# Three more block products in the first FFN of a two-layer trunk, and the side work moved for them

## The chip, the cores and the metric

The kernel runs on one core of a Trainium2 chip, in one launch. The metric is the device time of one execution in microseconds (us), the median of several runs. All arithmetic is float32; the matrix products are made of parts in a rounded format ("hi" and "lo" of each operand), three passes per product.

## The reference

Two layers, each of a mixer (attention, a convolution module and a short gated convolution side by side) and an FFN, on 528 positions (16 meta tokens and 512 inputs) of width 1024. The part that the change touches is the FFN of the first layer:

```python
def ffn_sublayer(h, pre_g, post_g, w_up, conv_w, w_down):
    u = rms_norm(h, pre_g)
    z = jnp.einsum("bld,df->blf", u, w_up)
    z = causal_depthwise_conv(z, conv_w)
    g, up = jnp.split(z, 2, axis=-1)
    y = jnp.einsum("blf,fd->bld", jax.nn.silu(g) * up, w_down)
    return h + rms_norm(y, post_g)
```

The hidden width is 2816, so `w_up` has 22 blocks of 128 columns for the gate and 22 for the other half, and `w_down` has 22 blocks of 128 rows.

## The kernel before

**Layout.** Activations lie with the features across the 128 partitions and the positions along the free side. A matmul has a 128x128 block of weights standing and at most 264 positions (half of 528) moving. Every weight block comes from DRAM by SP's queue into a `raw` buffer (three of them in a ring), is rounded by ScalarE into `whi`, and VectorE makes `wlo = raw - whi` (L652 and L653 in `prep_one`). The product of a block is whi*uhi, whi*ulo and wlo*uhi. `next_w` keeps two blocks split ahead of the one in use.

**The FFN in three parts.** The 22 pairs (gate block f and up block f) are done in parts of 8, 7 and 7 (`PARTS`). In a part, the pairs are multiplied, put through the convolution of three taps, silu and product (`ffn_gate`, which ends with VectorE's `y` at L2191), and then the part's gates go through their share of `w_down`, eight chunks of 128 columns: the part's down product. A plain pair is 96 matmuls (two blocks, 8 row blocks, 3 passes, 2 halves); a down product of the first part in the first layer is 384.

**Seven instead of eight.** Some pairs are made by `seven_pair`. Rows of weights, gate and up, and the two halves of the positions give a 2x2 by 2x2 block product, and seven products of blocks do it in place of eight: 7 x 4 row blocks x 3 passes = 84 matmuls (L2288 in `product`). They need sums of activations, four tiles `t` made by `normalised` in steps that `build` lets out during the first part (five behind each of pairs 2 to 6, in order) and during the first down product; a `None` in the steps ends a call. And they need sums of weight blocks, `w_sum` in DRAM, which are made long before the pair, in one of these ways:

- by DMA: three copies from DRAM to DRAM from SP's queue (L545), then three DMAs of POOL's queue that add into DRAM (L534), each behind the one before (`sum_steps`). In the mixer they are operations of the plan, at the lowest priority (8), with `SUM_LAT` as the planned time to landing and `SUM_EVERY` between two sums. In the FFN, `tick` lets out one step per pair.
- on VectorE, during a down product, in the tile of h as a spare (`down_sum`, L589 to L601).

Which pair is made when is in `SUMS`: for each layer five places, namely the FFN before (for layer 0 nothing), the mixer, the FFN's ticks, the first and the second down product.

**The spare.** Behind the first part h isn't needed until the FFN's end. It is copied to DRAM (`h_dram`, L2385), its tile serves as four more raw buffers, and it is read back later.

**Blocks split ahead.** While layer 0's FFN runs, six blocks of layer 1's input projection are split and put into DRAM as hi and lo, so that layer 1's mixer needn't split them. `store_one` does it in seven calls: each splits the block that the call before loaded (ScalarE L666 into `shi`, VectorE L667 into `slo`, one buffer each, then two stores from POOL's queue at L670), and all but the last load another (SP, L675). `shi` and `slo` also serve the block products.

**Order.** In the mixer and at the FFNs' ends the order on PE, ACT, DVE and POOL is written out by a planner (`Flow`) that has costs per operation; an operation with a priority number of 4 or more gives way there to one that is ready soon. In the rest of the FFN, and on SP's queue everywhere, the tile framework sets each queue's order by simulating the program, so that an instruction may be issued ahead of its place in the code; `issue_after` ties one instruction behind another of its engine. Each engine works its own queue strictly in order.

```python
for b in (b12, b22, b11, b21):
    for k in range(K2):
        yield lambda b=b, k=k: un(b, k)
for k in range(0, K2, 2):
    if k:
        yield None
```

Of the kernel before, what the change touches and what calls it, by code (L numbers as in the profile page):

```python
# [28 lines left out]
PARTS = (8, 7, 7)  # L29


SUMS = (((), (11, 12, 13), (15, 16), (17, 18), (19, 20)),
        ((8, 9), (10, 11, 12, 13), (15, 16), (17, 18), (19, 20)))
SEVEN = tuple(sorted(sum(places, ())) for places in SUMS)
NEXT_SUMS, AHEAD_SPLITS = 13, (8, 8, 9, 9, 10, 10, 11)
SUM_US, SUM_LAT, SUM_EVERY = 0.9, 9.0, 40.0
K2 = KD // 2
SB = K2 * P
AHEAD = 2
# [350 lines left out]
def tile_hybrid_trunk(ctx: ExitStack, tc: tile.TileContext, xT, wflat, pv_d, out):  # L390
# [734 lines left out]
    def mixer(l, ypool, first, close_first, spans, front, rzs, u_at):  # L1125
# [719 lines left out]

        for i, f in enumerate(sums_at(l, 1)):
            copies, *adds = sum_steps(l, f)
            tok = flow.op("sp", 2.0, copies, (Tok(flow.pe + SUM_EVERY * i),), prio=8, lat=SUM_LAT)
            for op in adds:
                tok = gp(SUM_US, op, tok, prio=8, lat=SUM_LAT)  # L1850

# [242 lines left out]
    for l in range(DEPTH):  # L2094
# [23 lines left out]
        with tc.tile_pool(name=f"fp{l}", bufs=2, reuse_waits="tile") as fp:  # L2118
# [91 lines left out]
            def normalised():  # L2210
# [39 lines left out]
                        yield lambda b=b, k=k: un(b, k)  # L2250
                for k in range(0, K2, 2):
                    if k:
                        yield None
                        yield lambda: block(0)
                        yield None
                    yield lambda: total(2, k, lambda: at(b12), lambda: at(b22))
                    yield lambda: split(2, k)
                    yield lambda: total(0, k, lambda: at(b11), lambda: at(b12))
                    yield lambda: total(1, k, lambda: at(b22), lambda: raw[0], ALU.add)
                    yield lambda: split(0, k)  # L2260
                    yield lambda: total(3, k, lambda: at(b21), lambda: raw[1])
                    yield lambda: split(1, k)
                    yield lambda: split(3, k)
# [4 lines left out]

            mul_ins, glo_ins, ghi_ins = [None], [None], {}
            ts, n_seven, primed = [], [0], set()  # L2270
            building = [None]

            def build(n):

# [64 lines left out]
            def finish_pair():  # L2339
                if late_ups:  # L2340
                    late_ups.popleft()()
# [3 lines left out]
            for part, nf in enumerate(PARTS):  # L2345
                for f in range(f0, f0 + nf):
                    if g:
                        tick(g[max(g)][0][:, :1])
                    for _ in range(AHEAD_SPLITS.count(f) if l == 0 else 0):
                        store_one()  # L2350
                    if f in seven:
                        seven_pair(f)
                        if f == seven[-1]:
                            spare[0] = None
                            with tc.issue_after(last_load[0].ins):
                                for k in range(0, KD, 2):
                                    nc.sync.dma_start(h[:, k:k + 2], h_dram[:, k:k + 2])
                        continue
                    finish_pair()
                    if seven and f == 2:  # L2360
                        building[0] = normalised()
                    for i in (2 * f, 2 * f + 1):
                        if i < len(zs):
                            continue
                        if i < FIRST["w_out"]:
                            scaled(i, [first.ps[hf, i] for hf in range(2)])
                            continue
                        w = next_w()
                        ps = mmt((6, 2)[i % 2]) if ts else mmt()
                        mm3({hf: ps[:, hf, :iws[hf]] for hf in range(2)}, w, range(KD), u_in)  # L2370
                        if ts:
                            for (a, z), hf in zip(i_spans, range(2)):
                                nc.scalar.copy(zs[i % len(zs)][:, off + a - i0:off + z - i0], ps[:, hf, :z - a])
                            continue
                        scaled(i, [ps[:, :, :H]] if i0 == 0 else [ps[:, hf, :iws[hf]] for hf in range(2)])
                    g[f] = ffn_gate(f)
                    if building[0] is not None and f < PARTS[0] - 1:
                        with tc.issue_after(mul_ins[0].ins):
                            build(5)
                finish_pair()  # L2380
                ks = list(range(nf))
                grhs = lambda b, k, hf, f0=f0: g[f0 + k][b][:, fw * hf:fw * (hf + 1)]
                if seven and part == 0:
                    for k in range(0, KD, 4):
                        nc.sync.dma_start(h_dram[:, k:k + 4], h[:, k:k + 4])  # L2385
                    spare[0] = h
                if part < len(PARTS) - 1:
                    more = down_sums(l, part)
                    for op in more.pop(-1):
                        op()  # L2390
                    for some in ((0, 1), *((m,) for m in range(2, KD))):
# [9 lines left out]
                        if building[0] is not None:  # L2401
                            with tc.issue_after(glo_ins[0].ins):
                                build(99)
                        for m, ps in zip(some, tiles):
                            if final:
                                d, src = yp[:, m, t0:], ps[:, 0, :2 * fw]
# [84 lines left out]
```

## Time and profile before

| | |
|---|---|
| time, median of 3 runs | 1263.06 us (1262.32 to 1263.31) |
| the profiled execution: time, span | 1262.1 us, 1260.4 us |
| TensorE (PE) busy | 1244.2 us, 99% of the span |
| VectorE (DVE) busy | 926.0 us, 73% |
| ScalarE (ACT) busy | 710.3 us, 56% |
| GpSimd (POOL) busy | 175.9 us, 14% |
| DMA | 206.59 MB, 164 GB/s in the mean |
| pairs made as block products | layer 0: 11, 12, 13, 15 to 20; layer 1: 8 to 13, 15 to 20 |

The span runs from the first to the last instruction of the profiled execution; its time is 1.7 us longer. In the rows, PE is a matmul, PEld its weight load, SP the queue of most DMAs; a q behind an engine's name is its queue or sequencer. "out<-in" are the program's tile names, L837 is line 837 of the kernel. An idle time in square brackets is the time that the engine stood still ahead of the row, and what ended it.

### The profile page before, as it was taken

The numbers are of one execution on the slowest core, as the hardware profiler recorded it, in microseconds if no ns is written. First come the engines' busy times: TensorE is split into PE (matmuls) and PEld (weight loads), VectorE is DVE, ScalarE is ACT, GpSimd is POOL, SyncE is SP. The second block draws the span as 40 slices with busy tenths as digits, with TensorE's granted clock in tenths as the row PEclk, the third lists the DMA queues.
The fourth block names the chain that finished last, engine by engine and source line by source line (L and its number), as shares of the span: only waits on it lengthen the run. The fifth ranks groups of instructions, "written<-read, shape, count | busy, mean of one in ns | idle before, by whom it ended". The sixth has DMA issues, their size and how long they took to land.

```text
span 1260.4 us, 24292 instructions
## 1 busy us (share of the span) xinstructions
PE 1244.2 (99%) x9554; PEld 1194.4 (95%) x9554; DVE 926.0 (73%) x1581; ACT 710.3 (56%) x1377; POOL 175.9 (14%) x360
## 2 busy tenths in 40 slices
PE   8999999999999999999999999999999999999997
PEld 8999898999999999999999988999999899989997
DVE  7887866589874776487688877756799748757954
ACT  7254576655444663476673545775554447526763
POOL 1323411001111001010003244110022000000000
PEclk9999999999999999999999999999999999999999
DMA  7267551726658755765652684547166565465611
GB/s 245 80 154 180 122 118 47 256 88 150 185 146 339 243 192 153 243 193 169 209 186 68 157 194 109 144 116 238 70 166 177 148 212 172 151 228 178 203 60 67
DMA packets 80755, 206.59 MB, mean 164 GB/s; under 512 B 8624, under 2 KB 18992, under 8 KB 80128
## 3 DMA queue, kind: packets, MB, share of 16 engines
q1 hardware_dynamic: 66976, 168.20, 42.1%
q0 software_dynamic: 13664, 36.84, 13.0%
q8 instruction: 75, 1.23, 0.4%
q14 instruction: 40, 0.33, 0.1%
HBM read 170.82 MB, written 50.60 MB: 176 GB/s over the span
## 4 chain that ended last, share of the span: by engine, by line
PE 94%; DVE 2%; ACT 1%; DMA 1%; POOL 1%; issue 0%; SPq 0%; DVEq 0%; ACTq 0%
PE psum L837 63%; PE psum L2288 17%; PE psum L1407 5%; PE psum L1671 3%; PE psum L1637 2%; PE psum L974 1%; PE psum L1593 1%; PE psum L1737 1%; PE psum L1323 1%; DMA raw<-in_w_dram 0%; POOL dm L1608 0%; DMA h<-in_x_dram 0%; DVE yp L1050 0%; DVE h L1060 0%; PE psum L1617 0%
## 5 line engine op out<-in xcount | busy, mean ns | idle before, releaser
L837 PE MATMUL psum<-y,whi 128*128 128x264 f32 (+3 forms) x1968 | 383.8, 299 | 0.8 <-DVE zs L989 0.7
L837 PEld LDWEIGHTS psum<-y,whi 128*128 128x128 f32 x1968 | 305.8, 188 | 13.7 <-DVE zs L989 0.9
L837 PE MATMUL psum<-uhi,whi 128*128 128x264 f32 (+1 forms) x1168 | 292.2, 289 | 1.5 <-ACT uhi L2069 0.8
L837 PE MATMUL psum<-ulo,whi 128*128 128x264 f32 (+1 forms) x1168 | 286.0, 284 | 0.6 <-DVE ulo L2071 0.4
L837 PE MATMUL psum<-uhi,wlo 128*128 128x264 f32 (+1 forms) x1168 | 285.3, 284 | 0.0
L837 PE MATMUL psum<-y,wlo 128*128 128x264 f32 (+3 forms) x984 | 274.0, 297 | 0.7 <-DVE wlo L793 0.7
L837 PEld LDWEIGHTS psum<-uhi,whi 128*128 128x128 f32 x1168 | 201.7, 189 | 5.9 <-issue 1.6
L837 PEld LDWEIGHTS psum<-ulo,whi 128*128 128x128 f32 x1168 | 201.8, 189 | 1.3 <-DVE ulo L2071 0.6
L837 PEld LDWEIGHTS psum<-uhi,wlo 128*128 128x128 f32 x1168 | 201.5, 189 | 0.0
L837 PEld LDWEIGHTS psum<-y,wlo 128*128 128x128 f32 x984 | 178.0, 188 | 6.4 <-DVE wlo L793 1.1
L2173 DVE SCALAR_TENSOR_TENSOR c<-zs,pv,c 128x528 f32<-128x528 f32 (+1 forms) x176 | 130.5, 756 | 21.2 <-ACT c L2171 19.9
L652 ACT CAST whi<-raw 128x1024 fp32r<-128x1024 f32 (+1 forms) x65 | 66.1, 1021 | 96.9 <-PE psum L837 74.3
L793 DVE TENSOR_TENSOR wlo<-raw,whi 128x1024 fp32r<-128x1024 f32 (+2 forms) x80 | 95.6, 1204 | 31.1 <-ACT whi L789 30.5
L789 ACT CAST whi<-raw 128x1024 fp32r<-128x1024 f32 (+2 forms) x80 | 81.7, 1030 | 26.3 <-PE psum L837 18.1
L653 DVE TENSOR_TENSOR wlo<-raw,whi 128x1024 fp32r<-128x1024 f32 (+1 forms) x65 | 76.9, 1183 | 20.9 <-ACT whi L652 20.9
L1153 DVE SCALAR_TENSOR_TENSOR cacc<-apad,pv,cacc 128x528 f32<-128x528 f32 x120 | 87.5, 771 | 0.1
L2288 PE MATMUL psum<-uhi,whi 128*128 128x258 f32 (+1 forms) x252 | 71.4, 284 | 0.0
L2288 PE MATMUL psum<-ulo,whi 128*128 128x258 f32 (+1 forms) x252 | 71.3, 283 | 0.0
L2288 PE MATMUL psum<-uhi,wlo 128*128 128x258 f32 (+1 forms) x252 | 70.8, 283 | 0.0
L2171 ACT ACTIVATE c<-zs,pv 128x528 f32<-128x528 f32 (+1 forms) x88 | 63.0, 727 | 6.8 <-DVE zs L2136 2.6
L2206 POOL COPY cols<-y 128x1 f32<-128x1 f32 x24 | 18.4, 767 | 334.7 <-ACT y L2187 334.4
L2288 PE MATMUL psum<-t,shi 128*128 128x258 f32 (+1 forms) x336 | 63.2, 283 | 0.0
(273 smaller groups left out, 2324.4 us busy)
## 6 DMA issues: line engine op xcount, KB each, us to landing
raw<-in_w_dram SPq DMA_DIRECT2D x114, 512.0 KB, 4.6
raw<-in_w_dram SPq DMA_DIRECT2D x30, 448.0 KB, 5.2
h<-in_w_dram SPq DMA_DIRECT2D x25, 512.0 KB, 4.7
raw<-w_sum SPq DMA_DIRECT2D x21, 512.0 KB, 5.2
h<-w_sum SPq DMA_DIRECT2D x21, 512.0 KB, 5.1
h<-in_w_dram POOLq DMA_DIRECT2D x16, 512.0 KB, 4.0
w_sum<-h POOLq DMA_DIRECT2D x16, 512.0 KB, 6.3
w_sum<-in_w_dram SPq DMA_DIRECT2D x26, 256.0 KB, 5.8
```

The lines of the kernel that those rows point to most:

```text
L652: nc.scalar.copy(hi[:, :sz], raw[:, :sz])
L653: last_low[0] = nc.vector.tensor_sub(lo[:, :sz], raw[:, :sz], hi[:, :sz].bitcast(F32))
L789: nc.scalar.copy(box["hi"][:, :sz], box["raw"][:, :sz])
L793: nc.vector.tensor_sub(lo[:, :sz], box["raw"][:, :sz], box["hi"][:, :sz].bitcast(F32))
L837: nc.tensor.matmul(d, lhsT=w[a][:, k, cols], rhs=rhs(b, k, hf), start=start and i == 0 and p == 0, stop=stop and i == n - 1 and p == 2)
L1153: nc.vector.scalar_tensor_tensor(conv[j], in0=src, in1=conv[j], scalar=col("a_dw_w", CK * j + i), op0=ALU.mult, op1=ALU.add)
L1407: nc.tensor.matmul(ps[:n, :nw], lhsT=(uhi, ulo)[ui][:, k, P * b:P * b + n], rhs=w[wi][:, k % 4, :], start=k == 0 and p == 0, stop=k == KD ...
L1637: nc.tensor.matmul(s, lhsT=k[:, ka:ka + kn], rhs=q[:, s0:qz], start=i == 0, stop=i == 1)
L1671: nc.tensor.matmul(acc[:, s0 - qa:qz - qa], lhsT=vals[:, b].rearrange("p h d -> p (h d)")[:, o:o + P], rhs=box["p"], start=b == 0, stop=b ...
L2171: nc.scalar.activation(dst, src[:, 2:2 + 2 * fw], AF.Copy, scale=wtap(2, t))
L2173: nc.vector.scalar_tensor_tensor(dst, in0=src[:, i:i + 2 * fw], scalar=wtap(i, t), in1=dst, op0=ALU.mult, op1=ALU.add)
L2288: nc.tensor.matmul(psum[:, bank, :n7], lhsT=w[a][:, k0 + k, :], rhs=rhs(b, k), start=start and k == 0 and p == 0, stop=stop and k == K2 - ...
```

## The change

- Layer 0's list gets pairs 8, 9 and 10. The mixer makes the sums of 8 to 12 (before: 11 to 13), the FFN's ticks those of 13, 15 and 16 (before: 15 and 16). Layer 1's list is the same.
- The seven calls of `store_one` stand at pairs 4, 5, 6 and 7 of layer 0 (one each), ahead of the first down product, and behind its first and second group of products. Before, they stood at pairs 8, 8, 9, 9, 10, 10 and 11.
- h is copied to DRAM at pairs 2 and 3, half each, in both layers. Before, behind the first part.
- `SUM_LAT` is 16 in place of 9, and the spacing of the sums is the lesser of 40 and 216 divided by their number.
- The `None` ahead of the second round of steps in `normalised` is left out once a part's pairs are done (`downs`).

```diff
-SUMS = (((), (11, 12, 13), (15, 16), (17, 18), (19, 20)),
+SUMS = (((), (8, 9, 10, 11, 12), (13, 15, 16), (17, 18), (19, 20)),
         ((8, 9), (10, 11, 12, 13), (15, 16), (17, 18), (19, 20)))
-NEXT_SUMS, AHEAD_SPLITS = 13, (8, 8, 9, 9, 10, 10, 11)
-SUM_US, SUM_LAT, SUM_EVERY = 0.9, 9.0, 40.0
+NEXT_SUMS = 13
+SUM_US, SUM_LAT, SUM_EVERY, SUM_SPAN = 0.9, 16.0, 40.0, 216.0
...
-            tok = flow.op("sp", 2.0, copies, (Tok(flow.pe + SUM_EVERY * i),), prio=8, lat=SUM_LAT)
+            tok = flow.op("sp", 2.0, copies, (Tok(flow.pe + min(SUM_EVERY, SUM_SPAN / len(sums_at(l, 1))) * i),), prio=8, lat=SUM_LAT)
...
                     if k:
-                        yield None
+                        if not downs:
+                            yield None
                         yield lambda: block(0)
...
-            building = [None]
+            building, downs = [None], []
...
-                    for _ in range(AHEAD_SPLITS.count(f) if l == 0 else 0):
+                    if l == 0 and PARTS[0] - 4 <= f < PARTS[0]:
                         store_one()
...
+                    if seven and f in (2, 3):
+                        k = 4 * (f - 2)
+                        nc.sync.dma_start(h_dram[:, k:k + 4], h[:, k:k + 4])
...
                 finish_pair()
+                downs.append(part)
...
                 if seven and part == 0:
-                    for k in range(0, KD, 4):
-                        nc.sync.dma_start(h_dram[:, k:k + 4], h[:, k:k + 4])
                     spare[0] = h
                 if part < len(PARTS) - 1:
+                    if l == 0 and part == 0:
+                        store_one()
...
+                        if l == 0 and part == 0 and some[0] in (0, 2):
+                            store_one()
```

## The prediction

> **What bounds the kernel now.** I read the page first, then the chain of waits in order of time, then busy time by stretches of the first FFN.
>
> ```profile
> span 1260.4 us, 24292 instructions
> PE 1244.2 (99%) x9554; PEld 1194.4 (95%) x9554; DVE 926.0 (73%) x1581; ACT 710.3 (56%) x1377; POOL 175.9 (14%) x360
> ...
> 276.51 134.52 PE psum L837 x1104
> 518.29 49.77 PE psum L2288 x410
> 983.08 39.83 PE psum L837 x171
> 1022.91 2.88 PE psum L2288 x24
> 1025.91 46.37 PE psum L2288 x386
> ...
> L2288 PEld LDWEIGHTS psum<-uhi,whi x252: 186/188/192, 434.4 to 1189.2; 128*128 128x128 f32 x126
> ```
>
> TensorE is busy for 99% of the span, and in both FFNs the chain is TensorE alone, in long pieces without a hole: L837 is the plain product, L2288 the block product. So a matmul taken out there is time taken out, as long as nothing else turns up late. The pieces give the pace: 134.52/1104 = 0.1219 us for a plain matmul, 49.77/410 = 0.1214 us for a block matmul of the first layer.
>
> The same pace dates the stages. The first block product of layer 0 starts at 434.4 (the last row, which tells first and last start). Before it lie pairs 8 to 10 (3x96 matmuls, 35.1 us, from 399.3), the first down product (384 matmuls, 46.8 us, from 352.5) and pairs 2 to 7 (11.7 us each, from 282.3). In these stretches:
>
> ```profile
> core 0: us, PE busy (x) PEld busy (x) DVE busy (x) ACT busy (x) POOL busy (x), PEclk, DMA share, GB/s
> ...
> 317.40:329.10 11.70, 11.70 (x98) 11.70 (x97) 9.96 (x15) 5.28 (x7) 1.52 (x3) 1.00 0.63 229
> 329.10:340.80 11.70, 11.70 (x98) 11.70 (x97) 10.69 (x15) 5.08 (x7) 2.14 (x3) 1.00 0.57 129
> 340.80:352.50 11.70, 11.70 (x98) 11.70 (x97) 10.74 (x15) 6.68 (x9) 1.36 (x2) 1.00 0.58 146
> 352.50:364.20 11.70, 11.70 (x98) 11.70 (x98) 6.75 (x9) 3.54 (x5) 1.39 (x2) 1.00 0.37 89
> 364.20:375.90 11.70, 11.70 (x99) 11.70 (x99) 11.30 (x15) 7.51 (x11) 1.15 (x2) 1.00 0.55 189
> 387.60:399.30 11.70, 11.70 (x99) 11.70 (x98) 3.68 (x3) 5.25 (x7) 1.59 (x3) 1.00 1.03 412
> 399.30:411.00 11.70, 11.70 (x99) 11.70 (x98) 4.62 (x4) 4.54 (x7) 1.60 (x3) 1.00 0.70 239
> ...
> 548.90:559.10 10.20, 10.20 (x86) 10.20 (x85) 8.86 (x13) 7.42 (x14) 1.31 (x1) 1.00 0.53 157
> ```
>
> The clock is 1.00 throughout. VectorE has about a microsecond free per pair in pairs 5 to 7 and more than half of the time at the end of the down product and in pair 8. Work is moved from the second place to the first, and that is the risk of this change.
>
> **The products.** Pairs 8, 9 and 10 of layer 0 become block products; pair 13 was one already and only its sums move. Removed: 288 x 0.1219 = 35.1 us. Added: 3 x 7 x 4 x 3 = 252 matmuls x 0.1214 = 30.6 us. Net **-4.5 us**. The two priming matmuls with ones are the same two. That twelve such pairs in this order can run without a hole is seen in layer 1, whose list is the same: its first down product ends at 983.08 + 39.83 = 1022.91, the first block product starts there, and 46 us follow with one break of 0.12 us.
>
> A block pair costs the other engines more: 3584 weight columns to split instead of 2048 and two more sums of psum. By the rows below (1.23 us for a split of 1024 columns, 0.71 for a psum step of 528) that is 1.8 + 2 x 0.4, some 2.6 us of VectorE. It lies beside TensorE, since a stretch of nothing but block pairs (548.90) has VectorE at 8.86 of 10.2 us; without that cover it would be 8 us for three pairs.
>
> **The hole before the first block product.**
>
> ```profile
> 434.47 1.05 ACT L652 CAST whi<-h 128x1024 fp32r<-128x1024 f32 x1 [0.59 <-PE psum L837]
> 436.07 0.64 ACT L2373 COPY zs<-psum 128x264 f32<-128x264 f32 x2
> 436.49 0.51 PE L2288 MATMUL psum<-t,whi 128*128 128x264 f32 x2 [0.35 <-ACT zs L2373]
> ```
>
> Today a plain pair stands just ahead of the first block pair, its last psum banks (2 and 3) are copied out behind a weight split, and the second block product waits for bank 2. After the change a down product stands there, as in layer 1, which has no such wait. **-0.4 us** (the idle time in the last row; bounds 0 and -0.4).
>
> **The six blocks split ahead** (`store_one`). Seven calls, as before: one load each but the last, then ScalarE's rounding, VectorE's rest, two stores from POOL's queue. They go from pairs 8 to 11 to pairs 4 to 7 (one each), the start of the down product and its first two steps.
>
> ```profile
> L666 ACT CAST shi<-raw 128x1024 fp32r<-128x1024 f32 x3 | 3.2, 1053 | 2.8 <-issue 2.5 <-DMA raw<-in_w_dram 0.3
> L667 DVE TENSOR_TENSOR slo<-raw,shi 128x1024 fp32r<-128x1024 f32 x3 | 3.7, 1225 | 7.0 <-DMA w_split<-slo 6.9
> L667 DVE TENSOR_TENSOR slo<-h,shi 128x1024 fp32r<-128x1024 f32 x3 | 3.7, 1224 | 7.9 <-issue 5.7 <-ACT shi L666 2.2
> ...
> 341.03 0.71 DVE L2136 TENSOR_TENSOR zs<-psum,rz 128x528 f32<-128x528 f32 x1 [0.78 <-PE psum L837]
> 352.76 0.71 DVE L2136 TENSOR_TENSOR zs<-psum,rz 128x528 f32<-128x528 f32 x1
> 358.15 0.71 DVE L2191 TENSOR_TENSOR y<-c,y 128x528 fp32r<-128x528 f32 x1 [0.70 <-ACT y L2187]
> ```
>
> Three splits fall in pairs 5 to 7: 3 x 1.23 = 3.7 us of VectorE, against 1.74 + 1.01 + 0.96 = 3.7 us free there. VectorE is then full. What is late next is pair 7's gate: its last VectorE step ends at 358.86, and the down product asks for it after 84 matmuls, at 352.5 + 10.2 = 362.7. Slack 3.8 us. If all free time is usable, VectorE is late by only the fourth split, 1.2 us; if none is, by 3.7 + 1.2 = 4.9 us. So TensorE loses 0 to 1.1 us. VectorE waits for psum rather than the reverse (0.78 at 341.03), and a psum pair has a whole chunk (5.85 us) before it is wanted again, so I take a value near the lower end, **+0.1 us**. ScalarE has half its time free. The last two splits fall in the down product, where VectorE has 5 us free at once (352.5 to 364.2).
>
> Each load now sits in the ring of three raw buffers, not in the spare one; weight loads lose one buffer of lead. Blocks are split two chunks (11.7 us) ahead of use, and a load lands in less than half of that:
>
> ```profile
> raw<-in_w_dram SPq DMA_DIRECT2D x114, 512.0 KB, 4.6
> w_split<-slo POOLq DMA_DIRECT2D x6, 512.0 KB, 6.5
> ```
>
> (KB each, median us from issue to landing). The six loads and twelve stores are 18 x 0.524 = 9.4 MB; the stretch of 387.6 moved 412 GB/s at share 1.03 with no hole in TensorE. At that rate they are 23 us of full load; spread over pair 5 to the middle of the down product (some 59 us) they add 0.39 to shares of 0.37 to 0.63: below what is carried today. Nothing charged; the price if a load or split is late after all is in the second rival.
>
> **The sums** (`w_sum`). Layer 0's mixer makes five instead of three, and SUM_LAT spaces their three POOL steps further apart, in both layers. What that costs is not seen before it is done; the nearest rows are layer 1's mixer with four and layer 0's with three, and the wait of a diagonal-matrix step on POOL that stood behind a sum's DMA:
>
> ```profile
> 49.50:214.00 164.50, 163.25 (x1216) 149.56 (x1214) 124.54 (x295) 94.54 (x246) 51.70 (x110) 1.00 0.50 119
> 675.50:840.80 165.30, 163.42 (x1219) 149.81 (x1217) 127.21 (x299) 94.88 (x245) 58.17 (x122) 1.00 0.56 131
> ...
> 115.56 0.39 PE L1617 MATMUL psum<-dm,ones_r 128*128 128x264 f32 x1 [0.43 <-POOL dm L1608]
> 742.23 0.40 PE L1617 MATMUL psum<-dm,ones_r 128*128 128x264 f32 x1 [0.98 <-POOL dm L1608]
> ...
> 200.00:220.00 20.00, 20.00 (x152) 18.41 (x151) 10.25 (x24) 12.86 (x35) 2.55 (x9) 1.00 0.12 38
> 220.00:240.00 20.00, 20.00 (x167) 20.00 (x166) 10.59 (x11) 14.07 (x22) 0.00 (x0) 1.00 0.82 281
> ```
>
> One more sum goes with 0.8 us at most. The fifth would be copied at about 210 and added up to 260, when POOL has nothing else to do. Its copies pass SP's queue ahead of the loads of h and of weights, 2 us of issue as the plan has it, which are wanted tens of microseconds later. Bounds: -1.4 us (both waits above gone) to +2.5 us (three new ones like 742's beside the 0.43). I take half of the 0.8, **+0.4 us**.
>
> **What changes nothing.** `SUM_SPAN`: min(40, 216/5) and min(40, 216/4) are both 40. The guard `if not downs`: pairs 2 to 6 take five steps each, the first run of steps has 16 + 8 = 24, so the pause falls in pair 6, where `downs` is still empty, in both layers. The copy of h, written earlier in the code, is issued early already, since outside the planned stages the order on a queue isn't the order of the code:
>
> ```profile
> 253.49 0.33 SPq L650 DMA_DIRECT2D raw<-in_w_dram  x1
> 266.52 6.02 SPq L2385 DMA_DIRECT2D h_dram<-h  x2
> 284.27 0.33 SPq L650 DMA_DIRECT2D raw<-in_w_dram  x1
> ```
>
> It lies in a stretch in which SP issues nothing else, some 80 us ahead of its place in the code (the end of pair 7, 352.5). Each at 0; if the copy moved in between weight loads, its 6 us would lie within their lead.
>
> **Sum.** -4.5 - 0.4 + 0.1 + 0.4 = -4.4 us: a span of 1260.4 - 4.4 = 1256.0. The profiled run took 1262.1 us, 1.7 beyond its span, and the median of the runs is 1263.06, another 0.96; on the median's scale **1258.7 us** (-0.35%). No change means within 0.2%, 2.5 us.
>
> **Rivals.**
>
> *VectorE stands behind the stores* (slower). `shi` and `slo` have one buffer each; the next split on VectorE waits, in order, until the last store has landed:
>
> ```profile
> 407.88 1.23 DVE L667 TENSOR_TENSOR slo<-h,shi 128x1024 fp32r<-128x1024 f32 x1 [5.66 <-issue]
> 415.54 1.22 DVE L667 TENSOR_TENSOR slo<-raw,shi 128x1024 fp32r<-128x1024 f32 x1 [2.66 <-DMA w_split<-slo]
> ...
> L534 POOL DMA_DIRECT2D w_sum<-w_sum x26: 796/844/890, 66.2 to 984.7; - x26
> ```
>
> There VectorE had nothing else to do. In pairs 5 to 7 everything behind it (psum copies, weights, gates) is late by the whole wait. Two waits like the first and the fourth split: 11.3 + 1.2 - 3.8 of slack = 8.7 us lost, 4.5 gained with the rest: +4.2, 1267.3. It turns the sign from 7.1 us of waiting on (7.1 + 1.2 - 3.8 = 4.5). Against it: the calls now come one to a pair, 11.7 us apart, and a store lands 6.5 us after issue, so it is through before the next split; before, calls came in twos. [...] Chance 0.10.
>
> *A late load or gate in the first part.* One wait of 5.66 with the fourth split: 5.7 + 1.2 - 3.8 = 3.1 us of the 4.5, so 1261.7. For it: VectorE full, a raw buffer less. Against: lead of 11.7 us. Chance 0.13, no change.
>
> *POOL's sums in the mixers.* Three waits like 742's more than now, 2.9 us in place of 0.4: 1261.2. For it: six more POOL steps in layer 0, and all steps of layer 1 at new places. Against: they yield to other work in the plan. Chance 0.12, about a third of it still faster.
>
> *More than forecast*: both waits above vanish, 1.4 and the 0.4 charged: 1256.9. Chance 0.07.
>
> *Forecast* (1257.4 to 1260.4): 0.58. Faster 0.58 + 0.07 + 0.04 = 0.69; no change 0.13 + 0.08 = 0.21; slower 0.10. The range 1256.9 to 1262.6 takes in the middle rivals and leaves out the slower one and a little below.
>
> **What would show it.** The first block product near 398 and no plain pair but 14 and 21 behind the first part; L667 once per pair from 317 on and VectorE at 11.5 of 11.7 us there, with psum copies never a chunk late. Wrong: a hole in TensorE ahead of 399 that ends with a gate or weight (stores), or more idle behind dm (sums), or h's copies elsewhere than in SP's empty stretch.

## The result and the profile after

The change made the kernel slower: 1274.92 us in the median of 4 runs (1272.62 to 1277.13) against 1263.18 for the kernel before beside it, a ratio of 1.0091 (95% interval 1.0067 to 1.0116). Forecast were 1258.7 us and a range up to 1262.6. The profiled execution took 1276.63 us, so its rows lie near the upper end of the runs. Three executions among the experiments below and beside them took 1502 to 3582 us; the ratios leave them out.

The page of the kernel after, its busy times and TensorE's granted clock in 40 slices:

```profile
span 1274.8 us, 24316 instructions
...
PE 1246.6 (98%) x9518; PEld 1195.4 (94%) x9518; DVE 931.7 (73%) x1593; ACT 716.1 (56%) x1389; POOL 184.2 (14%) x373
...
PEclk9998999999989999999999999999999999999999
```

The matmuls are the 36 fewer that were forecast (9518 against 9554), and yet PE is busy for longer and the span is 14.4 us longer. The clock row, all nines before, has two eights (slices at 96 and 351 us). The chain of waits in order of time dates the loss. First the kernel before, three rows beside those already shown:

```profile
211.37 1.57 PE psum L837 x12
...
690.09 6.95 PE psum L837 x57
...
840.79 31.19 PE psum L837 x261
```

and the kernel after:

```profile
218.72 1.57 PE psum L837 x12
...
350.83 12.13 DMA w_split<-slo
...
527.99 49.77 PE psum L2289 x410
699.75 6.95 PE psum L837 x57
...
854.83 31.19 PE psum L837 x261
```

The same piece of layer 0's mixer comes at 218.72 and not 211.37: **7.35 us** were lost before it. The third part's block products begin at 527.99 and not 518.29: 9.70 behind, so the first FFN lost 2.35 on balance (with the 5.1 us that the products are worth, shown below, **7.4 us**). Layer 1's mixer begins as late as that (699.75 against 690.09) and ends 14.04 behind (854.83 against 840.79): **4.4 us** more. Behind it nothing changes much: 14.4 at the end.

**The two mixers.** What POOL issues, and when TensorE comes back, in the timeline of after:

```profile
102.06 0.87 POOL L534 DMA_DIRECT2D w_sum<-w_sum  x1
...
104.04 0.74 POOL L534 DMA_DIRECT2D w_sum<-in_w_dram  x1
...
114.11 0.49 PE L1593 MATMUL psum<-k,q 128*16 128x16 f32 x2 [4.08 <-issue]
...
748.64 0.50 PE L1593 MATMUL psum<-k,q 128*16 128x16 f32 x2 [3.42 <-issue]
```

The same stretch before has one sum's DMA in place of two:

```profile
101.19 1.19 POOL L534 DMA_DIRECT2D w_sum<-in_w_dram  x1
```

SP issues four copies of k at some 106.8 in both. The DMA view of that stretch (KB each, median us from issue to landing), of after:

```profile
k<-pair_hi SPq DMA_DIRECT2D x4, 132.0 KB, 7.0
```

and of before:

```profile
k<-pair_hi SPq DMA_DIRECT2D x4, 132.0 KB, 2.6
```

SP's queue (q1) and POOL's (q0) in that stretch of after, with packets, MB and the share of the 16 DMA engines' time:

```profile
q1 hardware_dynamic: 1058, 2.08, 48.3%
q0 software_dynamic: 416, 0.79, 41.0%
```

With 16 us as the planned time of a step, the last step of the first sum falls to 102.06, next to the first step of the second sum. Two sums' DMAs are then in flight when k's copies are issued, these land after 7.0 us in place of 2.6, and TensorE stands for 4.08 us. Layer 1 has the same at 745.2 (3.42). For each MB that the profile counts, the sums on POOL's queue take more than twice the engines' time of SP's transfers (41.0/0.79 = 52 against 48.3/2.08 = 23).

**The first down product.** The timeline of after, POOL, ScalarE, VectorE and TensorE:

```profile
349.38 1.22 POOL L534 DMA_DIRECT2D w_sum<-in_w_dram  x1
350.83 0.58 POOL L670 DMA_DIRECT2D w_split<-slo  x1 [0.23 <-DVE slo L667]
...
359.64 1.05 ACT L666 CAST shi<-raw 128x1024 fp32r<-128x1024 f32 x1 [4.16 <-DMA raw<-in_w_dram]
...
363.04 1.23 DVE L667 TENSOR_TENSOR slo<-raw,shi 128x1024 fp32r<-128x1024 f32 x1 [5.57 <-DMA w_split<-slo]
364.18 0.70 DVE L2184 TENSOR_TENSOR c<-c,c 128x528 f32<-128x528 f32 x1
...
365.60 0.73 PE L837 MATMUL psum<-y,whi 128*128 128x264 f32 x3 [3.01 <-ACT y L2187]
367.31 0.59 PE L837 MATMUL psum<-y,wlo 128*128 128x264 f32 x1 [0.98 <-DVE wlo L653]
```

The fourth split (349.31) stands ahead of pair 5's last VectorE step (`y`, 350.45). Its store is issued 1.5 us behind a sum's DMA on POOL's queue and takes 12.1 us (the chain's 12.13). The fifth split needs `slo` and stands next in VectorE's order, so VectorE waits for 5.57 us with the rest of pair 6's gate behind it (L2184 at 364.18), and TensorE, which began the down product at 360.26 and asks for pair 6 after 18 matmuls, for 3.01 and then for 0.98. A late load has a smaller part in it: the split's other input `shi`, for which ScalarE waited 4.16 us, was ready at 359.64 + 1.05 = 360.69, and the store alone held VectorE for the 2.35 us from there to 363.04.

By the code the fifth split belongs behind the down product's first products, and two splits lie ahead of pair 6's gate. In VectorE's order it is five: the six splits run at 305.6, 324.6, 337.6, 349.3, 363.0 and 376.3, one ahead of each `y` of pairs 2 to 7 (313.0, 326.9, 339.9, 350.4, 368.5, 380.3). The framework's simulation of the program put them there.

**The clock.** Each of the three holes is paid twice. Six stretches of after, in the columns known from the prediction (PEclk is the third number from the end):

```profile
109.00:115.00 6.00, 1.92 (x14) 1.74 (x13) 1.63 (x7) 0.39 (x1) 0.27 (x1) 0.87 1.01 207
115.00:121.00 6.00, 6.00 (x31) 6.00 (x31) 2.60 (x12) 1.52 (x3) 1.16 (x4) 0.56 0.13 35
361.00:367.00 6.00, 2.32 (x17) 1.80 (x15) 3.96 (x5) 4.35 (x6) 2.33 (x4) 0.92 0.56 167
367.00:373.00 6.00, 5.69 (x26) 5.69 (x27) 6.00 (x10) 1.90 (x3) 0.07 (x1) 0.52 1.08 240
744.00:750.00 6.00, 2.58 (x18) 2.40 (x17) 1.87 (x7) 0.39 (x1) 0.51 (x2) 0.86 0.97 223
750.00:756.00 6.00, 5.58 (x39) 5.37 (x39) 3.91 (x11) 2.22 (x4) 2.29 (x4) 0.86 0.26 67
```

From 115 to 121 TensorE is busy all the time and gets 31 matmuls done; before, at a clock of 1.00, 6 us of the same stage (109 to 115) have 50. The clock lost is (0.13 + 0.44) x 6 = 3.4 us, (0.08 + 0.48) x 6 = 3.4 and (0.14 + 0.14) x 6 = 1.7: 8.5 us in all, on top of 4.1, 4.0 and 3.4 us of standing still. Together 20 us, near the 7.35 + 7.4 + 4.4 = 19.2 of the chain (in layer 1 the wait for `dm` became 0.6 us shorter, 0.42 in place of 0.98). In slices of 1 us the granted clock is 0.50 from 114 to 120, from 366 to 372 and from 749 to 751, with values between 0.50 and 1.00 in a slice just before or behind: the losses of 3.4, 3.4 and 1.7 us are some 6.8, 6.8 and 3.4 us at half clock. They don't follow the holes' length: 3.01 us, with 0.98 behind it, cost as much as 4.08, and 3.42 half of that.

### The profile page after: what moved, and what is told of

Its sections match the earlier page's. It is cut to its first block, busy times and chain, and to the rows that moved or that the text cites. A ratio compares the mean times of both kernels' runs of the same rounds, so it can differ in the third digit from the quotient of the medians.

```text
span 1274.8 us, 24316 instructions
## 1 busy us (share of the span) xinstructions
PE 1246.6 (98%) x9518; PEld 1195.4 (94%) x9518; DVE 931.7 (73%) x1593; ACT 716.1 (56%) x1389; POOL 184.2 (14%) x373
## 4 chain that ended last, share of the span: by engine, by line
PE 85%; DMA 5%; DVE 4%; issue 2%; ACT 2%; POOL 1%; SPq 0%; DVEq 0%; ACTq 0%; POOLq 0%
PE psum L837 52%; PE psum L2289 19%; PE psum L1407 4%; DMA raw<-in_w_dram 3%; PE psum L1671 3%; PE psum L1637 2%; PE psum L974 1%; DMA w_split<-slo 1%; PE psum L1593 1%; PE psum L1737 1%; PE psum L1323 1%; DVE wlo L793 1%; ACT whi L789 1%; SPq L494 0%; DMA h<-in_x_dram 0%
## 5 line engine op out<-in xcount | busy, mean ns | idle before, releaser
L837 PE MATMUL psum<-uhi,whi 128*128 128x264 f32 (+1 forms) x1072 | 273.1, 290 | 1.7 <-ACT uhi L2069 0.8
L837 PE MATMUL psum<-ulo,whi 128*128 128x264 f32 (+1 forms) x1072 | 266.8, 285 | 0.6 <-DVE ulo L2071 0.4
L837 PE MATMUL psum<-uhi,wlo 128*128 128x264 f32 (+1 forms) x1072 | 265.9, 285 | 0.0
L837 PEld LDWEIGHTS psum<-uhi,whi 128*128 128x128 f32 x1072 | 187.9, 190 | 6.3 <-issue 2.0
L837 PEld LDWEIGHTS psum<-ulo,whi 128*128 128x128 f32 x1072 | 187.9, 190 | 1.3 <-DVE ulo L2071 0.6
L837 PEld LDWEIGHTS psum<-uhi,wlo 128*128 128x128 f32 x1072 | 187.5, 190 | 0.0
L653 DVE TENSOR_TENSOR wlo<-raw,whi 128x1024 fp32r<-128x1024 f32 (+1 forms) x64 | 75.6, 1181 | 11.8 <-ACT whi L652 11.8
L2289 PE MATMUL psum<-uhi,whi 128*128 128x264 f32 (+1 forms) x288 | 81.6, 284 | 0.0
L2289 PE MATMUL psum<-ulo,whi 128*128 128x264 f32 (+1 forms) x288 | 81.4, 283 | 0.0
L2289 PE MATMUL psum<-uhi,wlo 128*128 128x264 f32 (+1 forms) x288 | 80.8, 283 | 0.0
L2289 PE MATMUL psum<-t,shi 128*128 128x264 f32 (+1 forms) x384 | 72.2, 283 | 0.0
L2206 POOL COPY cols<-y 128x1 f32<-128x1 f32 x28 | 20.3, 725 | 337.6 <-ACT y L2187 337.4
```

The lines of the kernel that those rows point to most:

```text
L653: last_low[0] = nc.vector.tensor_sub(lo[:, :sz], raw[:, :sz], hi[:, :sz].bitcast(F32))
L837: nc.tensor.matmul(d, lhsT=w[a][:, k, cols], rhs=rhs(b, k, hf), start=start and i == 0 and p == 0, stop=stop and i == n - 1 and p == 2)
L2289: nc.tensor.matmul(psum[:, bank, :n7], lhsT=w[a][:, k0 + k, :], rhs=rhs(b, k), start=start and k == 0 and p == 0, stop=stop and k == K2 - ...
```

## The experiments

"Hole" is idle time of TensorE. The kernel before took 1262.7 to 1263.8 us beside these runs.

**One part on the old kernel: the planned time of a sum's step.**

```diff
-SUM_US, SUM_LAT, SUM_EVERY = 0.9, 9.0, 40.0
+SUM_US, SUM_LAT, SUM_EVERY = 0.9, 16.0, 40.0
```

> The kernel before with SUM_LAT 16 alone: three sums in layer 0 and four in layer 1, only POOL's order differs. Theory: both mixers get their hole and half clock, +11.3 us: 1274.5. Rival (number of sums): layer 0 has no hole with three sums, at most layer 1's +4.1: 1267.3 or 1263.2.

1271.82 us, ratio 1.0060 (1.0043 to 1.0077): some 8 us from this number alone, with three sums in layer 0 and four in layer 1. Its timeline has the two steps side by side, and both holes (the second at 741). Behind the first the granted clock is 0.96 from 109 to 115 and 0.76 from 115 to 121, (0.04 + 0.24) x 6 = 1.7 us:

```profile
101.80 0.87 POOL L534 DMA_DIRECT2D w_sum<-w_sum  x1
...
103.78 0.74 POOL L534 DMA_DIRECT2D w_sum<-in_w_dram  x1
...
113.22 0.34 PE L1593 MATMUL psum<-k,q 128*16 128x16 f32 x2 [3.43 <-issue]
```

So the mixers' loss comes from the spacing, not from the fifth sum.

**The other part on the old kernel: the stores' new place.**

```diff
-                    for _ in range(AHEAD_SPLITS.count(f) if l == 0 else 0):
+                    if l == 0 and PARTS[0] - 4 <= f < PARTS[0]:
                         store_one()
...
+                    if l == 0 and part == 0:
+                        store_one()
...
+                        if l == 0 and part == 0 and some[0] in (0, 2):
+                            store_one()
```

> The kernel before with one part of the change alone: the seven calls that split weights ahead stand in pairs 4 to 7 and at the head of the first down product; sums, spacing and pairs are as before. Theory (the stores' new place makes the hole by itself, because a store waits in POOL's queue behind a sum's DMA and VectorE waits for the store): no hole in the mixers, a hole of 3 to 4.5 us at the first down product and 6.8 us at half clock behind it, so 1263.8 + 4.4 + 3.4 = about 1271. Rival (the hole needs what the three further pairs bring: the sum steps of pair 13 in the first part and the early copy of h): no hole, 1263.5 to 1264.5.

1269.16 us, ratio 1.0045 (1.0030 to 1.0060): about 6 us, and 1.8 us less than the 1271 expected, which had 3.4 us of half clock in it. (The four executions had a mean clock of 0.997 to 1.000, so they didn't all lose as much clock.) Its chain of waits has the same step as after's:

```profile
341.32 2.07 POOL w_sum L534
343.63 12.33 DMA w_split<-slo
```

The hole needs nothing of what the three pairs bring. How long a store takes varies: 3.0 us is the fastest of before, 6.5 us is the median of the `slo` stores of before, and 12.1 and 12.3 us are these two, with a sum's DMA of 512 KB just ahead in the queue.

**Undo one part of after: the spacing back at 9 us.**

```diff
-SUM_US, SUM_LAT, SUM_EVERY, SUM_SPAN = 0.9, 16.0, 40.0, 216.0
+SUM_US, SUM_LAT, SUM_EVERY, SUM_SPAN = 0.9, 9.0, 40.0, 216.0
```

> The changed kernel with SUM_LAT back at 9: the order of every engine's queue but POOL's stays as it is. Theory (two causes that add up): with 16 the third step of the mixer's first sum and the first step of its second stand within 2 us ahead of k's copies, these land late, TensorE stands still for 4.4 us in layer 0 and 3.7 us in layer 1, and its clock is at half for 6.8 and 3.4 us after; both holes go with 9, worth 7.2 + 4.1 = 11.3 us: 1263.6. Rival (it is the number of sums, five, that overloads the mixer of layer 0, not their spacing): only layer 1's hole goes, 1270.8.

1278.14 us, ratio 1.0117 (1.0096 to 1.0137), against every expectation. The two holes ahead of k go, but with five sums a new one opens at 206.8, the longest of all:

```profile
204.59 1.15 POOL L534 DMA_DIRECT2D w_sum<-in_w_dram  x1 [5.05 <-DMA w_sum<-in_w_dram]
214.72 0.85 POOL L534 DMA_DIRECT2D w_sum<-w_sum  x1 [8.97 <-DMA w_sum<-in_w_dram]
...
215.92 0.80 PE L1671 MATMUL psum<-pf,vals 128*128 128x128 f32 x2 [9.10 <-POOL pf L1651]
```

POOL waits in order for the landing of the step before (10 us, planned as 9) and holds attention's `pf` behind it. This is the event that the prediction looked for (TensorE idle behind POOL), in a size that it did not have.

**Undo the other part of after: the stores at their old places** (pairs 8, 8, 9, 9, 10, 10 and 11, the diff above backwards), alone and together with 9 us.

> The changed kernel with the calls of store_one back at pairs 8, 8, 9, 9, 10, 10, 11, SUM_LAT still 16. Theory: the hole in the first down product (4.8 us and 6.8 us at half clock after it) goes, 7.4 us: 1267.5, with the two holes of the mixers still there. Rival (the first part is late because of the sums of three more pairs, not because of the stores): the hole stays, 1274.9. Second rival (the stores in among block pairs, with one shi and slo for both, make a new hole at pairs 8 to 11): 1270 or more.

> The changed kernel with both undone: only the three more block pairs, their two sums and the inert edits are left. Theory: no hole of three microseconds, clock at 1.0 throughout, and the block products' 4.5 us are gained: 1258.7 (1257.5 to 1260.5). Rival (five sums or stores among block pairs cost what the products gain): 1263 or more.

1302.83 us, ratio 1.0306 (1.0291 to 1.0322), and 1302.99, ratio 1.0315 (1.0298 to 1.0332). Both expectations were far off: the pairs there are block pairs now, which split into the same `shi` and `slo`. The chain of the first of the two runs:

```profile
442.74 5.27 DMA w_split<-shi
...
452.31 6.67 DMA w_split<-slo
```

These two waits end in holes of 4.85 and 3.03 us. Two more, of 3.4 and 3.2 us, lie between 424 and 480, and in the 6 us from 426, 450, 456 and 476 the granted clock was 0.82, 0.52, 0.78 and 0.63. So the stores had to move once pairs 8 to 10 were block products; what failed is the place that they got.

**Fewer sums at 9 us.**

```diff
-SUMS = (((), (8, 9, 10, 11, 12), (13, 15, 16), (17, 18), (19, 20)),
+SUMS = (((), (9, 10, 11, 12), (13, 15, 16), (17, 18), (19, 20)),
...
-SUM_US, SUM_LAT, SUM_EVERY, SUM_SPAN = 0.9, 16.0, 40.0, 216.0
+SUM_US, SUM_LAT, SUM_EVERY, SUM_SPAN = 0.9, 9.0, 40.0, 216.0
```

> The kernel after with the planned time of a sum's step back at 9 us and with pair 8 plain again, so four sums in layer 0's mixer and eleven pairs as block products. Theory (five sums were too many for the mixer's stretch at 9 us, and four are not): no hole over 1.5 us in either mixer; the hole at the first down product stays (about 4.4 us and 6.8 us at half clock); products worth two thirds of 4.5: 1263.8 - 3.0 + 7.8 = about 1268.5. Rival (any sum beyond the third meets POOL's other work): a hole of 5 to 9 us in layer 0's mixer with half clock behind it, 1275 or more.

1267.43 us, ratio 1.0032 (1.0019 to 1.0045), within 1.1 us of the theory: no hole over 0.6 us in layer 0's mixer or over 1.2 in layer 1's, and the hole at the first down product stays.

**The steps of the sums kept away from the stores.**

```diff
-                    if g:
+                    for _ in range((0, 2, 2, 2, 0, 0, 0, 0)[f] if l == 0 and f < 8 else min(1, len(g))):
                         tick(g[max(g)][0][:, :1])
```

> The kernel after, with the sums' steps of layer 0's first part two in each of pairs 1 to 3 and none in pairs 4 to 7, where the stores stand. Theory (the store of pair 7 is late because it stands behind a sum's DMA in POOL's queue): the stores land in 4 to 6 us, the hole at the first down product goes with its half clock, the two mixer holes stay: 1274.9 - 7.4 = about 1267.5. Rival (the raw loads are late because loads and stores together fill the DMA engines, whoever shares the queue): the hole stays within 1 us, 1274 to 1276.

1277.54 us, ratio 1.0119 (1.0096 to 1.0142): the time fits the rival, but the timeline shows the theory's mechanism at another place. A double step stands ahead of a store there, the store takes 8.2 us, and the second split waits for it:

```profile
323.42 1.23 DVE L667 TENSOR_TENSOR slo<-raw,shi 128x1024 fp32r<-128x1024 f32 x1 [8.30 <-issue]
...
326.09 0.48 PE L837 MATMUL psum<-uhi,whi 128*128 128x264 f32 x2 [2.58 <-DVE zs L2136]
...
367.13 0.63 PE L837 MATMUL psum<-y,whi 128*128 128x264 f32 x3 [1.38 <-ACT y L2187]
```

At the fifth split VectorE no longer waits for a store, and of the 4.0 us of hole behind it 1.8 stay (1.38, and 0.39 a little later). There it waits for ScalarE, 4.62 us at 362.13, and that waits for a late `raw` load. That fits the reading of after, in which the store held VectorE for 2.35 us longer than the late load. It isn't a clean test of the shares, since TensorE is some 3 us later here and the loads had that much more time.

**Stores not in every pair.** As the run with four sums, and:

```diff
-                    if l == 0 and PARTS[0] - 4 <= f < PARTS[0]:
+                    for _ in range((4, 6, 8, 8).count(f) if l == 0 else 0):
                         store_one()
```

> As the run with four sums and 9 us, but the seven calls that split ahead stand at pairs 4 and 6, three at the first down product as after, and two at pair 8, which is plain here. Theory (the hole at the first down product comes from stores in every one of pairs 4 to 7): no hole of 3 us anywhere, no half clock, 1263.8 - 3.0 + 0.4 = about 1261.2. Rival (two stores are enough for the hole there, or pair 8's stores delay the first block products): a hole of 3 to 4 us and 3.4 or 6.8 us at half clock at one of the two places, 1266 to 1269.

1260.20 us in 10 runs, ratio **0.9979 (0.9969 to 0.9988)**: 3.1 us less than the kernel before beside it, a small gain that the interval sets apart from none. No hole over 0.9 us up to layer 1's mixer, none over 1.7 behind it. Against the run with four sums alone the stores' place is worth 1267.4 - 1260.2 = 7.2 us.

**Five sums, and the stores apart.** The next four runs keep all twelve pairs. Three have the stores at pairs 4 and 6, around the first down product's head, and in the second down product:

```diff
-                    if l == 0 and PARTS[0] - 4 <= f < PARTS[0]:
+                    if l == 0 and f in (4, 6):
                         store_one()
...
-                        if l == 0 and part == 0 and some[0] in (0, 2):
+                        if l == 0 and (part, some[0]) in ((0, 0), (0, 2), (1, 2), (1, 6)):
                             store_one()
```

They differ in the planned time of a step: 16 us as in after, 12 and 13. The fourth has 13 us and after's stores.

> The kernel after with the seven calls that split ahead at pairs 4 and 6, three at the first down product and two in the second; the planned time of a sum's step stays at 16 us. Theory (the losses are separate and add): both mixer holes stay with their half clock, the hole at the first down product goes: 1274.9 - 7.2 = about 1267.7, up to 1270. Rival: without the stores in every pair the mixers' holes are worth what they are alone in the kernel before (8.0 us), 1259.2 + 8.0 = 1267.2; much below that, the holes of after would have had a common cause.

1268.47 us, ratio 1.0052 (1.0034 to 1.0070): the down product's hole is gone (TensorE is busy for all of 361 to 373 there, at a clock of 1.00), both mixer holes stay. 6.5 us better than after.

> The kernel after with the planned time of a sum's step at 12 us, between the 9 of before and the 16 of after, and with the seven calls that split ahead at pairs 4 and 6, three at the first down product as after, and two in the second down product (at its row blocks 2 and 6). All twelve pairs stay block products. Theory (both holes come from where POOL's DMAs fall, not from the twelve pairs): with 12 us the planner puts other POOL work between a sum's DMAs ahead of k's copies and leaves no pf behind the sums; no hole over 1.5 us, no half clock, 1263.3 - 4.5 + 0.4 = about 1259.2. Rival (no spacing carries five sums; the DMA engines are full): a hole of 3 us or more in layer 0's mixer with 3.4 to 6.8 us at half clock, 1264 or more. A hole in the second down product would speak against the stores there alone.

> As the run with 12 us, but 13 us. Theory: the same, about 1259.2, as long as no two sum DMAs stand side by side ahead of k's copies; the second step of the first sum falls later than at 12, nearer to the first pair of q's copies, so up to 1 us of hole may show there. Rival (the time follows the spacing itself, 9 to 16): between the two, a k hole of 2 to 3 us in each mixer, 1263 to 1266.

1269.15 us, ratio 1.0052 (1.0036 to 1.0067), and 1267.88, ratio 1.0040 (1.0025 to 1.0055). Both theories fell: no hole over 2 us ahead of k, but one of about 4 us near the mixer's end. The chain of the run with 13 us, and the group of TensorE that came late:

```profile
227.93 9.73 DMA raw<-in_w_dram
```

```profile
217.90 1.46 POOL L534 DMA_DIRECT2D w_sum<-in_w_dram  x1
...
253.34 1.25 PE L974 MATMUL psum<-acc,om_d 128*128 128x264 f32 x2 [4.12 <-DVE acc L934]
```

The fifth sum now falls where h and the output weights are loaded, a load takes 9.73 us, and the weights behind it stay late up to the norm. That its DMAs are the cause is likely by place and time; no run took them alone away.

> The kernel after with the planned time of a sum's step at 13 us and nothing else changed. Theory (the two losses are separate and add): the mixers' holes are gone, the hole at the first down product stays: the run with 13 us and moved stores plus 7.2 us (what the same stores cost with four sums), so about 1266.4. Rival (the holes in the first part come from the mixer ending late): none at the down product, the same time as with moved stores.

1271.22 us, ratio 1.0073 (1.0047 to 1.0099): both holes are there, the mixer's end and the down product's (4.64 us, and 3.93 and 0.68). The rival is out; the 1266.4 presumed a mixer without a hole. The stores cost 3.3 us here, less than the 7.2 between the two runs with four sums; why is open.

**Each sum where none was seen to cost.** 9 us (`SUM_LAT` as before) for the first two sums of layer 0 and for layer 1, 16 for layer 0's last three; stores as in the three runs that have them apart:

```diff
-            tok = flow.op("sp", 2.0, copies, (Tok(flow.pe + min(SUM_EVERY, SUM_SPAN / len(sums_at(l, 1))) * i),), prio=8, lat=SUM_LAT)
+            tok = flow.op("sp", 2.0, copies, (Tok(flow.pe + min(SUM_EVERY, SUM_SPAN / len(sums_at(l, 1))) * i),), prio=8, lat=SUM_LAT if l or i < 2 else 16.0)
             for op in adds:
-                tok = gp(SUM_US, op, tok, prio=8, lat=SUM_LAT)
+                tok = gp(SUM_US, op, tok, prio=8, lat=SUM_LAT if l or i < 2 else 16.0)
```

> All twelve pairs as block products, the stores apart as in the runs with 12 and 13 us, and the planned time of a sum's step 9 us for the first two sums of layer 0's mixer and for all of layer 1's, 16 us for layer 0's last three. POOL's order is then that of the kernel before up to the second sum and that of after behind it. Theory (each loss is where a sum's DMAs fall, not the number of sums): no hole over 1.5 us, no half clock, 1262.7 - 4.5 + 0.4 + up to 1 for the two stores in the second down product = 1258.6 to 1260. Rival (five sums do not fit the mixer's stretch at any spacing): a hole of 3 us or more somewhere between 109 and 255 us, 1265 or more.

1263.01 us in 11 runs (1258.34 to 1267.05), ratio 1.0002 (0.9989 to 1.0016). The rival fell: five sums, and no hole over 0.8 us in layer 0's mixer. Each of 9, 12, 13 and 16 us for all of them had left one of 3.8 us or more there. The time was above the theory, with one hole of 1.77 us behind the second down product. The chain ahead of it goes through a sum's copy and a load, and the clock falls behind it:

```profile
492.96 9.06 DMA w_sum<-h
...
510.50 6.77 DMA h<-in_w_dram
```

```profile
516.00:522.00 6.00, 4.23 (x25) 4.01 (x24) 1.45 (x2) 2.01 (x4) 0.00 (x0) 0.78 0.71 232
522.00:528.00 6.00, 6.00 (x48) 6.00 (x48) 3.34 (x4) 4.10 (x6) 0.00 (x0) 0.93 0.23 80
```

**The two stores out of the second down product.**

```diff
-                    if l == 0 and f in (4, 6):
+                    if l == 0 and f in (2, 4, 6):
                         store_one()
...
-                        if l == 0 and (part, some[0]) in ((0, 0), (0, 2), (1, 2), (1, 6)):
+                        if l == 0 and part == 0 and some[0] in (0, 2, 6):
                             store_one()
```

> As the run with 9, 9, 16, 16 and 16 us, but the two calls that split ahead in the second down product are moved: the seven stand at pairs 2, 4 and 6, before the first down product and at its row blocks 0, 2 and 6. Theory (the 1.94 us hole behind the second down product and the spread of 1258.3 to 1267.1 us come from the stores there, which stand ahead of the sums' DMAs in POOL's queue): no hole over 1.5 us, no half clock, a spread like the kernel before's, 1262.9 - 4.5 + 0.4 = 1258.8 to 1259.5. Rival (the hole is the sums' own, a late load at the first block product of the third part): a hole of 1.5 to 2.5 us there again, 1262 to 1263.5; a hole in the first down product, about 1266, would say that its head carries no more stores than three.

1260.26 us in 11 runs (1258.22 to 1262.41), ratio **0.9974 (0.9965 to 0.9983)**: all twelve pairs, and again 3.1 us less than the kernel before. That hole is gone, and there is no half clock. Its chain in order of time, and below it that of the run with four sums and stores at 4, 6, 8 and 8:

```profile
277.19 122.83 PE psum L837 x1008
...
513.90 49.77 PE psum L2289 x410
```

```profile
276.94 52.79 PE psum L837 x432
...
515.82 49.77 PE psum L2289 x410
```

From the FFN's long chain to the third part's block products it is 518.29 - 276.51 = 241.78 us before, 236.71 here and 238.88 with eleven pairs: 5.07 and 2.90 us less. Both runs end 3.1 us below the kernel before in the median, so the twelfth pair's 2.2 us aren't seen in the time. In the profiled executions most of them are lost in layer 1: 0.6 us in its mixer, and 1.2 in a hole at the start of its third part's block products that the run with eleven pairs doesn't have. Over all executions the median of the spans is 4.2 us below before with twelve pairs (1257.5 against 1261.7) and 3.2 with eleven (1258.4 against 1261.6). So 1.0 us of the pair is there, and the time beyond the span, 1.7 us in the kernel before, is 2.6 to 4.2 us in five of the eleven executions with twelve pairs. Why that is so stays open.

## Why the prediction was wrong, step by step

**The products and the hole before the first block product: right.** -4.5 and -0.4 were forecast, 5.07 were measured where nothing else was late, and 2.90 for two pairs (two thirds of 4.5, with a plain pair still ahead). The first block product starts at 403.20 - 24 x 0.12 = 400 in the last run; the forecast was 398, though the prediction's own dates put the end of the down product at 399.3. In after itself the gain is not to be seen alone, since the holes lie on top of it.

**What changes nothing: right as far as it was seen.** The copy of h, written earlier in the code, is issued at 274.22 in after and at 266.52 in before, 7.7 us later like all around it, in the same empty stretch of SP. That `SUM_SPAN` and the guard do nothing rests on the prediction's arithmetic; no run changed them alone.

**The stores: wrong, +0.1 became 7.4 us** with after's spacing (7.2 between the two runs with four sums, about 6 on the old kernel). The step that failed is in the first rival: "the calls now come one to a pair, 11.7 us apart, and a store lands 6.5 us after issue, so it is through before the next split". The single buffer was right, two things were not. The 6.5 us was a median of six stores, of 4.4 to 8.4 us, none of which stood behind a DMA that adds into DRAM; in the first part the sums' steps share POOL's queue, and the store that mattered took 12.13 us. And "three splits fall in pairs 5 to 7" took the calls at their place in the code, though the order of an engine's queue isn't that of the code here: five splits stood ahead of pair 6's gate, and that gate, which the prediction didn't look at, was the late one. The prediction had this in hand: it uses it for the copy of h, and its own rows of 407.88 and 415.54 are the fourth and fifth split of before, which by the code belong to pair 10, at 422.7. So the mechanism of the rival that the prediction gave a tenth is what happened, with one wait of 5.57 us in place of two, and one gate sooner; the length of the hole, 3.01 us, is close to the 3.1 of its rival of a late gate (0.13), which leaves out the clock as well. The DMA forecast beside it failed too, though its share was right: at most 0.63 + 0.39 was expected, "below what is carried today", and ahead of the hole it was 1.00:

```profile
355.00:361.00 6.00, 6.00 (x52) 6.00 (x51) 2.46 (x4) 1.84 (x3) 0.01 (x1) 1.00 1.00 295
```

The step that failed is the rate. At that share 295 GB/s were moved here and not 412, so the transfers took longer than counted, and a raw load was late by 4.16 us.

**The sums in the mixers: wrong, +0.4 became 7.35 + 4.4 = 11.8 us.** The failing step is the bound: it was drawn from `dm`, what POOL's own work waits for behind a sum. The wait that came was SP's: k's copies, 2.6 us grown to 7.0 beside two sums' DMAs. No row of before shows that, since there the two never stood together; the upper bound of +2.5 was a bound on the wrong resource. And it was a constant, not the new sums, that moved them together: the same 16 us costs 8 us on the old kernel. The constant couldn't just have stayed, though: at 9 us the five sums make a hole of 9.10 us.

**Missing altogether: the clock.** Every rival priced a hole by its length. Each of these cost 1.7 to 3.4 us more, 8.5 us in sum, well over the gain that was forecast. The clock row of before, 1.00 throughout, stood for a kernel without a hole, and the rivals were holes. They were also priced one at a time, and two of them came together.

The sum as measured: -5.1 + 7.4 + 7.35 + 4.4 = 14.1, against 14.4 of span (the first two are one measured number, 2.35, with the products' part taken from the last run).

## What to carry to other kernels

Price a hole on TensorE as its length plus what the half clock behind it costs, 1.7 or 3.4 us for the three holes of 3.0 to 4.1 us in the kernel after: that can double the bill. Count an engine's slack in the order in which the trace shows its work, not in the order of the code. Take a DMA's time to landing from the queue and the neighbours that it will have, not from the median of where it stood (12.1 us here, by a median of 6.5). And a planner's constant that stands for a landing time places every operation behind it: change it only for those that need it, as the last run's 9, 9, 16, 16 and 16 us do.

## What the runs showed of the hardware

The holes of 3.0 us and more in the stretches above had half clock behind them: 4.08, 3.01 and 3.42 us in the kernel after cost 3.4, 3.4 and 1.7 us of clock, and 3.43 us in the old kernel with 16 us cost 1.7. Around the 9.10 us of the run at 9 us with five sums the clock was 0.87, 0.50 and 0.77 in the three stretches of 6 us from 206. Two shorter holes differ: 1.67 us ahead of k in the run with 13 us left the clock at 1.00 from 109 to 121, but 1.77 us in the run with 9 and 16 us cost (0.22 + 0.07) x 6 = 1.7 us of clock, by the two stretches shown there. The two rows:

```profile
111.69 0.34 PE L1593 MATMUL psum<-k,q 128*16 128x16 f32 x2 [1.67 <-issue]
```

```profile
518.46 0.39 PE L2289 MATMUL psum<-uhi,whi 128*128 128x264 f32 x1 [1.77 <-ACT whi L652]
```

Unexpected: how much later copies landed beside two DMAs that add in DRAM than beside one. Four copies of 132 KB on SP's queue took 7.0 us beside two such DMAs on POOL's (after) and 2.6 beside one (before), the 7.0 in a stretch (109 to 115) with the 16 engines at a share of 1.01 and 207 GB/s; the prediction's stretch of 387.6 moved 412 GB/s at 1.03.
